# RMS norm and matmul on one core: TensorE's program as two pages, with a first pass through both

## The chip, the cores and the metric

The kernel runs on one core of a Trainium2 chip. The metric is the device time of one execution in microseconds (us). The profile is one execution taken by the hardware profiler; its span runs from the first to the last profiled instruction.

The engines are TensorE (PE; PEld is its weight load, which overlaps with products), VectorE (DVE), ScalarE (ACT), GpSimd (POOL) and SyncE (SP), whose queue issues nearly all transfers. Sixteen DMA engines carry them; each transfer is split over all sixteen.

## The reference

```
batch, seq, dim, out_dim = 16, 1024, 512, 768
rms = sqrt(mean(x ** 2, axis=-1, keepdims=True) + eps)
x_norm = x / rms * gamma
return matmul(x_norm, weight)
```

x has 16,384 rows of 512 floats (33.6 MB), the output 16,384 rows of 768 (50.3 MB). All is float32.

## The kernel before

**Tiles.** A tile is 128 rows, and there are NT = 128 tiles, worked in NP = 64 pairs j. x is loaded in groups of up to 16 tiles into two buffers xt, the results leave from three buffers ot in stores of up to 8 tiles. For each pair:

- POOL casts x to bf16 (`cast`, line 251, into xb; `cast_quad`, line 326, into xq).
- ACT squares and sums the rows (`square`, line 258) and takes the root; DVE forms the reciprocal (`root`, line 265).
- The tiles have to be turned so that features lie across the partitions. Six pairs of eight are turned on PE (`transpose_word`, line 292: four words of 128x128 for a pair, into PSUM tp) and copied out by DVE (`evac`, line 301, into xT). The last two pairs of each group of eight, from pair 14 on, are turned by DVE alone (`move_quad`, line 342, sixteen moves, three at a time, into xTq). Pairs 6 and 7 are turned on PE, too, but land in xTq.
- PE multiplies by the weights, which gamma has been folded into (`matmuls`, line 373: four weight loads and eight products a tile). Between the products `feed` puts the transposes of a later pair (`feeder`, line 396, with a list of how many words follow each of the eight weight loads).
- `finish_tile` (line 385) scales by the reciprocal on its way out of PSUM, the even tile of a pair on ACT, the odd one on DVE, and `store` (line 355) issues the transfer once the tiles of a store are there.

**Order of issue.** Nothing is scheduled by a tool. Every operation is recorded with `run` or `order.transfer` in the order in which the code stands, and `Order.emit` (line 37) then works out which waits each one needs, gives out semaphores and issues it on its engine. The main loop over pairs (line 473) lists loads, casts, norms, products.

PE's instructions as the built program has them, transposes counted as a weight load and a product: 240 in the opening, 242 in the loop, 49 behind it.

## Time and profile before

| what | value |
|---|---|
| median of 3 runs (lowest to highest) | 209.61 us (209.57 to 210.52) |
| the profiled execution, its own time | 210.62 us |
| its span | 208.8 us |
| bytes read from and written to HBM | 35.13 MB, 50.33 MB |
| last products on PE end, last eviction starts | 199.40 us, 199.44 us |
| a turn of PE's loop (eight pairs) | 23.4 us |

How to read it: the page gives busy time by engine, the span in 40 equal slices with the busy share in tenths, the DMA queues (q1 carries the kernel's transfers, the queues of the kind "instruction" the loading of program pages), and groups of instructions by line. The views by stretches give busy time of PE, PEld, DVE, ACT and POOL, the granted clock of PE, the mean busy share of the DMA engines and what they moved. A mean over DMA engines does not tell whether all of them work; how far apart they are is read from the landing records, sixteen for each transfer.

### The profile page before, as it was taken

Reading aid. Unit: us, or ns where it says so; the run is one execution under the profiler, and the core shown is the slowest. Engines: PE = TensorE matmul, PEld = TensorE weight load, DVE = VectorE, ACT = ScalarE, POOL = GpSimd, SP = SyncE. Lnnn points to the kernel's source line nnn. Section 1 sums busy time; section 2 is a strip of 40 time slices with the busy share of each in tenths; the row PEclk is TensorE's granted clock in tenths of the full one; section 3 lists DMA queues with packets and bytes.
Section 4 is the critical chain, followed back from the end, with each engine's and each line's share of the span. In section 5 each row is a group of like instructions: output and inputs, shape, how many; then the busy total and the mean of one; then the engine's idle time right before and its main releaser. Section 6 shows DMA issues by size and latency. Waiting matters only on the chain.

```text
span 208.8 us, 2821 instructions
## 1 busy us (share of the span) xinstructions
PE 194.5 (93%) x1236; PEld 72.7 (35%) x717; DVE 149.4 (72%) x255; ACT 146.2 (70%) x363; POOL 59.8 (29%) x34
## 2 busy tenths in 40 slices
PE   7789979999999999999999999999999999999910
PEld 1234433443344333342344333443333334433200
DVE  0455645999569975999469984999569984999410
ACT  4698888677877498774977787677877688673310
POOL 3147633009300093004900651006700265000000
PEclk9999999999999999999999999999999999999995
DMA  6999999999999999999999999999999999999991
GB/s 227 426 439 430 377 385 430 477 405 430 405 388 414 369 438 424 454 402 449 428 413 446 408 450 428 414 438 425 443 433 414 452 408 438 438 433 400 420 414 78
DMA packets 5628, 85.55 MB, mean 410 GB/s; under 512 B 626, under 2 KB 628, under 8 KB 1780
## 3 DMA queue, kind: packets, MB, share of 16 engines
q1 hardware_dynamic: 5616, 85.46, 97.4%
q8 instruction: 3, 0.05, 0.1%
q14 instruction: 5, 0.04, 0.0%
q10 hardware_dynamic: 4, 0.00, 0.0%
HBM read 35.13 MB, written 50.33 MB: 409 GB/s over the span
## 4 chain that ended last, share of the span: by engine, by line
PE 71%; DMA 15%; DVE 6%; issue 2%; SPq 1%; ACT 1%; POOL 1%; ACTq 0%
PE ps L367 62%; DMA xt<-in_x_dram 15%; PE ps L296 8%; DVE ot L350 2%; DVE xTq L340 2%; DVE xT L309 1%; POOL xb L254 1%; ACT jk L262 0%; SPq L416 0%; SPq L243 0%; ACT ot L348 0%; DVE xTq L309 0%; SPq L360 0%; DVE rstd L269 0%; SPq L544 0%
## 5 line engine op out<-in xcount | busy, mean ns | idle before, releaser
L367 PE MATMUL ps<-w_bf,xT 128*128 128x512 bf16 (+1 forms) x768 | 141.8, 326 | 1.4 <-DVE w_bf L350 0.9
L348 ACT ACTIVATE ot<-ps,rstd 128x768 f32<-128x768 f32 x64 | 57.4, 897 | 42.4 <-PE ps L367 41.2
L262 ACT ACTIVATE jk<-xt 128x512 bf16<-128x512 f32 x128 | 78.7, 618 | 6.9 <-DMA xt<-in_x_dram 6.9
L254 POOL CAST xb<-xt 128x2048 bf16<-128x2048 f32 (+3 forms) x21 | 46.2, 2218 | 114.5 <-DMA xt<-in_x_dram 95.7
L350 DVE TENSOR_SCALAR ot<-ps,rstd 128x768 f32<-128x768 f32 x64 | 64.8, 1013 | 9.0 <-PE ps L367 8.4
L363 PEld LDWEIGHTS <-xT 128*128 128x128 bf16 x384 | 37.7, 98 | 58.2 <-issue 56.9
L296 PE MATMUL ps<-ident_f,xb 128*128 128x128 f32 x200 | 54.2, 275 | 0.9 <-POOL xb L254 0.9
L340 DVE STREAM_TRANSPOSE xTq<-xq 32x256 f32<-32x256 f32 x112 | 48.8, 435 | 3.4
L367 PE MATMUL ps<-w_bf,xTq 128*128 128x512 bf16 (+1 forms) x256 | 49.0, 326 | 1.2 <-DVE xTq L309 1.2
L309 DVE COPY xT<-ps 128x1024 bf16<-128x1024 bf16 (+1 forms) x51 | 33.1, 652 | 23.1 <-PE ps L296 21.5
L296 PEld LDWEIGHTS ps<-ident_f,xb 128*128 128x128 f32 x200 | 28.4, 143 | 46.2 <-issue 42.9
L262 ACT ACTIVATION_READ_ACCUMULATOR jk<-xt 128x1 f32 x128 | 24.3, 190 | 0.0
L363 PEld LDWEIGHTS <-xTq 128*128 128x128 bf16 x128 | 12.5, 98 | 17.8 <-issue 16.1
L329 POOL CAST xq<-xt 128x2048 bf16<-128x2048 f32 x7 | 13.3, 1893 | 0.0
L269 DVE RECIPROCAL rstd<-rms 128x8 f32<-128x8 f32 (+3 forms) x20 | 3.9, 193 | 8.0 <-ACT rms L267 7.8
L267 ACT ACTIVATE rms<-ssq,eps_sb 128x8 f32<-128x8 f32 (+3 forms) x20 | 6.0, 300 | 0.6
L367 PE MATMUL ps<-warm 128*128 128x512 bf16 x10 | 4.4, 578 | 1.4 <-DVE eps_sb L425 1.4
L394 ACT ACTIVATE told<-eps_sb 128x1 f32<-128x1 f32 x20 | 3.8, 192 | 0.0
L309 DVE COPY xTq<-ps 128x1024 bf16<-128x1024 bf16 x2 | 1.4, 692 | 2.4 <-PE ps L296 2.4
L348 ACT ACTIVATE w_bf<-w_f,g_sb 128x768 bf16<-128x768 f32 x2 | 1.9, 935 | 1.5 <-DMA w_f<-in_weight_dram 0.9
L446 DVE COPY g_sb<-ps 128x4 f32<-128x4 f32 x1 | 0.2, 161 | 3.2 <-PE ps L440 3.2
L412 ACT ACT_TABLE_LOAD x1 | 1.3, 1283 | 1.5 <-SPq L503 1.5
(12 smaller groups left out, 3.6 us busy)
## 6 DMA issues: line engine op xcount, KB each, us to landing
out_dram<-ot SPq DMA_DIRECT2D x13, 3072.0 KB, 16.3
xt<-in_x_dram SPq DMA_DIRECT2D x9, 2048.0 KB, 21.0
xt<-in_x_dram SPq DMA_DIRECT2D x3, 4096.0 KB, 22.1
out_dram<-ot SPq DMA_DIRECT2D x4, 1536.0 KB, 12.0
out_dram<-ot SPq DMA_DIRECT2D x3, 768.0 KB, 8.2
w_f<-in_weight_dram SPq DMA_DIRECT2D x2, 768.0 KB, 5.7
xt<-in_x_dram SPq DMA_DIRECT2D x2, 512.0 KB, 5.2
xt<-in_x_dram SPq DMA_DIRECT2D x1, 1024.0 KB, 9.2
```

The source lines that it names most:

```text
L254: run(POOL, lambda: POOL.tensor_copy(out=xb[s][:, i % 8:i % 8 + n, :], in_=src), of, cells("xb", s, i % 8, n))
L262: run(ACT, lambda: ACT.activation(out=jk[j], in_=src[:, 0, :], func=AF.Square, accum_out=ssq[:, i:i + 1]), of, [("jk", j), ("ssq", i)])
L267: run(ACT, lambda: ACT.activation(out=rms[:, s], in_=ssq[:, s], func=AF.Sqrt, scale=1.0 / D, bias=eps_sb), [("ssq", t) for t in range(i, i ...
L269: run(DVE, lambda: DVE.reciprocal(out=rstd[:, s], in_=rms[:, s]), [("rms", i)], [("rstd", t) for t in range(i, i + n)])
L296: run(PE, lambda: PE.transpose(out=tp[b][:, t, h, :], in_=words[:, lo:lo + P], identity=ident_f), cells("xb", s, j % 4 * 2 + t) + ["ident" ...
L309: run(DVE, lambda: DVE.tensor_copy(out=dst[:, t:t + n, :], in_=src[:, t:t + n, :]), [("tp", b)], to[t:t + n])
L329: run(POOL, lambda: POOL.tensor_copy(out=xq[s], in_=src), of, [("xq", s)])
L340: run(DVE, lambda: DVE.transpose(out=dst, in_=src), [("xq", s)], ["xTq"])
L348: run(ACT, lambda: ACT.mul(out=dst, in_=src, mul=r), reads, writes)
L350: run(DVE, lambda: DVE.tensor_single_scalar(out=dst, in_=src, scalar=r, op=mybir.AluOpType.mult), reads, writes)
L363: run(PE, lambda: PE.ldweights(lhsT), [cell])
L367: run(PE, lambda: PE.add_instruction(mybir.InstMatmult(name=nc.get_next_instruction_name(), engine=mybir.EngineType.PE, ins=[PE.lower_ap(r ...
```

## The change

- **The loop begins at pair 4 and takes in the last pair.** Its turns are pairs 4 to 11, 12 to 19 and so on, and the last one is only its first half, pairs 60 to 63: a counter `turn` is compared in the middle of each turn, and the last turn leaves there. Nothing stands behind the loop.
- **Opening.** It now holds pairs 0 to 3 only. So that the loop's body is the same in each turn, pairs 3 and 4 are transposed during pair 2, pairs 5, 6 and 7 (12 words) during pair 3, and no words during pairs 4 and 5.
- **Transposes at the end.** Pairs 62 and 63 feed pairs 64 and 65, which don't exist: the words of an old xb are transposed, and not copied out.
- **Two stand-ins.** A memset of one column on POOL at pair 60 and one on DVE at pair 5 are recorded as if they wrote xb and xTq, so that each turn has the same waits.
- **A first pass.** All of PE's program lies in an outer loop of two passes. In the first, `seen` is 0: it branches past the opening, then past the loop to the code behind it, and back. In the second it runs both.
- **Warm-up.** The first warm-up of PE has five products instead of six.

Before has 240, 242 and 49 PE instructions in the three parts; after has 182 in the opening (with its branch), 113 and 130 in the loop's two halves, and four in what follows.

```
@@ Order.emit
-        assert all([h for _, h in self.body[t]] == [h for _, h in self.body[turns[0]]] for t in turns)
-        waits = [sorted({place[d][0] for t in turns for d in needs[self.body[t][q][0]]}) for q in range(size)]
+        middle = sum(h == 0 for _, h in self.body[turns[0]])
+        assert all([h for _, h in self.body[t]] == [h for _, h in self.body[turns[0]]] for t in turns[:-1])
+        assert [h for _, h in self.body[turns[-1]]] == [0] * middle
+        waits = [sorted({place[d][0] for t in turns for d in needs[self.body[t][q][0]]} if q < middle else
+                        {place[d][0] for t in turns[:-1] for d in needs[self.body[t][q][0]]}) for q in range(size)]
...
-            q = next(q for q in range(final + 1, size) if q not in flags and q not in taken and self.ops[self.body[turns[0]][q][0]][0] == "product")
+            q = next(q for q in range(final + 1, (middle, size)[half]) if q not in flags and q not in taken and self.ops[self.body[turns[0]][q][0]][0] == "product")
...
-        behind = max(spot)
-        late = [n for n in outer if n > behind and self.ops[n][1] is nc.tensor]
+        only = [mybir.EngineType.PE]
+        opening = [n for n in outer if self.ops[n][1] is nc.tensor]
+        assert max(opening) < min(spot)
         for n in outer:
-            if n < len(self.ops) - 1 and n not in late:
+            if n < len(self.ops) - 1 and self.ops[n][1] is not nc.tensor:
                 give(n)
-        with nc.Fori(0, len(turns), engines=[mybir.EngineType.PE], head_slot={mybir.EngineType.PE: 0}):
-            for q, (n, half) in enumerate(self.body[turns[0]]):
-                for who in waits[q]:
-                    nc.tensor.wait_ge(own[who, half], values[q, who])
-                ins = self.ops[n][2]()
...
-        for n in late:
-            give(n)
+
+        def part(name, above):
+            nc.switch_body(name, parent=above, valid_engines=only)
+
+        seen, turn = (nc.alloc_registers(name, engines=only) for name in ("seen", "turn"))
+        nc.regs_mov(seen, 0)
+        with nc.Fori(0, 2, engines=only):
+            above = nc.cur_bb.parent
+            nc.br_lt(seen, 1, on_true="past_opening", on_false="opening", engines=only)
+            part("opening", above)
+            for n in opening:
+                give(n)
+            nc.br("past_opening", engines=only)
+            part("past_opening", above)
+            nc.br_lt(seen, 1, on_true="past_turns", on_false="turns", engines=only)
+            part("turns", above)
+            nc.regs_mov(turn, 0)
+            with nc.Fori(0, len(turns), engines=only, head_slot={mybir.EngineType.PE: 0}):
+                within = nc.cur_bb.parent
+                for q, (n, half) in enumerate(self.body[turns[0]]):
+                    if q == middle:
+                        nc.br_lt(turn, len(turns) - 1, on_true="second_half", on_false="past_turns", engines=only)
+                        part("second_half", within)
+                    for who in waits[q]:
+                        nc.tensor.wait_ge(own[who, half], values[q, who])
+                    ins = self.ops[n][2]()
...
+                nc.regs_alu(turn, turn, 1, op=mybir.AluOpType.add)
+            nc.br("past_turns", engines=only)
+            part("past_turns", above)
+            nc.regs_alu(seen, seen, 1, op=mybir.AluOpType.add)
@@ feeder
-                elif (t, h) == (1, 1):
+                elif (t, h) == (1, 1) and j < NP:
                     evac(j)
@@ ahead of the pairs
-    warm_up(6)
+    warm_up(5)
@@ the loop over pairs
-    mid, one, two, both = ([0, 0, 1, 1, 0, 1, 1, 0], [1, 1, 0, 1, 1, 0, 0, 0], [1, 0, 1, 0, 1, 0, 1, 0],
-                           [1, 1, 1, 1, 1, 1, 1, 1])
+    mid, two, both, most = ([0, 0, 1, 1, 0, 1, 1, 0], [1, 0, 1, 0, 1, 0, 1, 0], [1, 1, 1, 1, 1, 1, 1, 1],
+                            [2, 1, 2, 1, 2, 1, 2, 1])
...
+        elif j % 8 == 4:
+            run(POOL, lambda: POOL.memset(warm[:, :1], 0.0), [], cells("xb", 0, 0, 8))
...
+        elif j == 5:
+            run(DVE, lambda: DVE.memset(warm[:, :1], 0.0), [], ["warm", "xTq"])
...
-        if j < 3:
-            feed = feeder([j + 1], mid if j == 1 else one, alone=j == 1)
+        if j == 1:
+            feed = feeder([2], mid, alone=True)
+        elif j == 2:
+            feed = feeder([3, 4], both)
         elif j == 3:
-            feed = feeder([4, 5], both)
-        elif j + 2 < NP and quad_of(j + 2) is None:
+            feed = feeder([5, 6, 7], most)
+        elif (j + 2) % 8 < 6:
             feed = feeder([j + 2], two)
...
-        order.turn, order.half = ((j - 6) // 8, (j - 6) % 8 // 4) if 6 <= j < NP - 2 else (None, 0)
+        order.turn, order.half = ((j - 4) // 8, (j - 4) % 8 // 4) if 4 <= j else (None, 0)
```

More of the change, by code (lines that the diff above doesn't have):

```diff
@@ L93, in emit @@
         for t in turns:
-            for half in range(2):
+            for half in range(2 if t != turns[-1] else 1):
                 for who in range(len(engines)):
@@ L116, in emit @@
         flags = {spot[d][1] for d in awaited if d in spot}
-        awaited |= {self.body[t][q][0] for t in turns for q in flags}
+        awaited |= {self.body[t][q][0] for t in turns for q in flags if q < len(self.body[t])}
         seen = {who for clock in known for who in clock}
@@ L145, in give @@
                 ins.then_inc(own[place[n][0], events[n][1]], 1)
-        behind = max(spot)
-        late = [n for n in outer if n > behind and self.ops[n][1] is nc.tensor]
+        only = [mybir.EngineType.PE]
+        opening = [n for n in outer if self.ops[n][1] is nc.tensor]
+        assert max(opening) < min(spot)
         for n in outer:
-            if n < len(self.ops) - 1 and n not in late:
+            if n < len(self.ops) - 1 and self.ops[n][1] is not nc.tensor:
                 give(n)
-        with nc.Fori(0, len(turns), engines=[mybir.EngineType.PE], head_slot={mybir.EngineType.PE: 0}):
-            for q, (n, half) in enumerate(self.body[turns[0]]):
-                for who in waits[q]:
-                    nc.tensor.wait_ge(own[who, half], values[q, who])
-                ins = self.ops[n][2]()
-                if n in marks:
-                    ins.then_inc(marks[n][0], 1)
-                elif q in taken:
-                    ins.then_inc(*taken[q])
@@ L161, in emit @@
-        for n in late:
-            give(n)
+        def part(name, above):
[22 more added lines that the diff above has]
+                    ins = self.ops[n][2]()
+                    if n in marks:
+                        ins.then_inc(marks[n][0], 1)
+                    elif q in taken:
+                        ins.then_inc(*taken[q])
+                nc.regs_alu(turn, turn, 1, op=mybir.AluOpType.add)
+            nc.br("past_turns", engines=only)
+            part("past_turns", above)
+            nc.regs_alu(seen, seen, 1, op=mybir.AluOpType.add)
```

## The prediction

> **What bounds the kernel now.** I read the page's shares and DMA lines first, then stretches of the span side by side, then TensorE's waits, then the DMA lines of three short stretches. By share PE looks like the bound (93% busy), but the transfers say otherwise.

> ```profile
> PE 194.5 (93%) x1236; PEld 72.7 (35%) x717; DVE 149.4 (72%) x255; ACT 146.2 (70%) x363; POOL 59.8 (29%) x34
> ...
> DMA  6999999999999999999999999999999999999991
> ...
> q1 hardware_dynamic: 5616, 85.46, 97.4%
> q8 instruction: 3, 0.05, 0.1%
> q14 instruction: 5, 0.04, 0.0%
> ```

> The sixteen DMA engines are full from the second slice to the last but one. Whole stretches run at some 430 GB/s, so 85.46 MB need 199 us, and the first data packet starts at 1.97 us (the trace's packet records). That leaves 208.8 - 201 = 8 us not accounted for. The next view (columns: stretch, its length, busy us of each engine, clock, DMA share, GB/s) shows where it is:

> ```profile
> 24.00:26.00 2.00, 2.00 (x15) 0.74 (x8) 0.99 (x2) 2.00 (x6) 1.50 (x1) 1.00 0.95 262
> 26.00:28.00 2.00, 2.00 (x15) 0.81 (x8) 0.62 (x1) 2.00 (x6) 0.00 (x0) 1.00 0.81 308
> ...
> 56.00:60.00 4.00, 4.00 (x28) 1.52 (x15) 2.58 (x4) 3.01 (x10) 0.00 (x0) 1.00 1.01 367
> ...
> 100.00:150.00 50.00, 50.00 (x327) 19.00 (x189) 39.37 (x66) 39.02 (x98) 18.66 (x9) 1.00 1.01 430
> ...
> 200.00:202.00 2.00, 0.00 (x0) 0.00 (x0) 0.46 (x1) 0.00 (x0) 0.00 (x0) 1.00 1.01 421
> 202.00:204.00 2.00, 0.00 (x0) 0.00 (x0) 0.00 (x0) 0.00 (x0) 0.00 (x0) 0.94 0.88 366
> 204.00:206.00 2.00, 0.00 (x0) 0.00 (x0) 0.00 (x0) 0.00 (x0) 0.00 (x0) 0.50 0.29 123
> 206.00:209.00 3.00, 0.00 (x0) 0.00 (x0) 0.00 (x0) 0.00 (x0) 0.00 (x0) 0.50 0.07 31
> ```

> Against 431 GB/s the dips cost 1.35 us in 24-28 and 0.6 us in 56-60. The tail matters more: from 204 on the DMA share is 0.29, then 0.07, so a few engines still work while most are done. A store is complete only when all sixteen have written their part. In the trace's records of the last store ten engines finish between 203.6 and 203.9 us, the other six at 204.64, 205.11, 205.88, 206.93, 207.40 and 207.56. **The end is set by the slowest DMA engine, 3.7 us behind the ten.**

> Following the same records back: up to the load that lands at 21.4 us no engine is over 0.5 us behind. In the load landing at 27.2 one is 2.0 us late; at 35.0 us two are 1.3 late; the pair stays together, 2.3 at 70, 3.2 at 119, 4.1 at 193. A third falls back slowly from about 80 us: its 24,576-byte packets of the stores take some 945 ns, the others' 912. TensorE's page loads fall into the same stretches. The first one stands at the loop's entry; PE's wait there (released by, us in total, times, longest) and the timeline around it:

> ```profile
> PE ps L367 <- DVE xTq L309: 1.2, 1, 1.2
> ...
> 28.04 0.69 DVE L309 COPY xTq<-ps 128x1024 bf16<-128x1024 bf16 x1 [1.42 <-PE ps L296]
> ...
> 29.52 0.50 PE L367 MATMUL ps<-w_bf,xTq 128*128 128x512 bf16 x2 [1.19 <-DVE xTq L309]
> ```

> The three packets of q8 are at 27.02, 33.03 and 194.14 us in the trace's records, 16,384 bytes each, 0.95 to 1.08 us long. The first two match the two laggards; after the third a new engine appears 1.8 us late. At the loop's entry PE is idle 1.19 us: the copy it is said to wait for ends at 28.73, yet PE resumes only at 29.52.

> **The change part by part.** The sum is made against the profiled execution: 210.62 us, of which 208.8 are span; the median of the runs, 209.61, is 1.01 lower, and I carry gains over to it.

> *Fewer page loads in the full stretch.* Before, 240 instructions of opening, then the loop's page, then 49 of late work. After, 182 of opening and one page that holds the loop, its exit and the end. The loads at 27.02 and 33.03 go, or move to about 1 us, ahead of the first x packets at 1.97. If both leaders of the queue of laggards lose their lag, the third sets the end, 206.93: 207.56 - 206.93 = **-0.63 us**. Bounds: 0, if an early load puts an engine as far behind, since nothing later lets it catch up; -3.7, if the others' lag goes as well. The load at 194.14 delays an engine that ends at 205.11 and is worth nothing by itself.

> *Loop entry.* The 1.19 us of PE go: pairs 6 and 7 are transposed at pair 3 already, and the loop starts at pair 4. PE is not the end, and the covering work is the DMA's backlog. Where PE's pace does reach DMA is early: the store issued at 50.11 comes 1.5 us before the one ahead of it lands (51.65), and DMA dips after it. An earlier store can close the dip at 56-60: **-0.6 us**. Bounds 0 (another cause) and -2.9 (this dip, the one at 24-28, and 1.0 us at 66-70, 324 GB/s). I take the one dip because it is the only one that follows a late store.

> *Dead transposes.* In the last half turn pairs 62 and 63 now feed pairs 64 and 65, which don't exist: 8 transposes at 0.108 us (their step between two products, 27.73 to 27.84) = 0.86 us on PE, nobody reads them. PE's net is -1.19 + 0.86, so the last eviction (199.44) moves by about -0.3. Cover: the lagging engines' backlog of 3.7 us. Without it the ten engines would be bare: the last store, issued at 200.8, plus 1.03 us from issue to first packet (x load, 0.94 to 1.97) plus 8 packets of 0.23 us ends at 203.7, just their end now. So 0, at most +0.9.

> *First pass.* Register moves and some six branches before the warm-up, which waits for VectorE until 1.40. Lower bound 0: five warm products instead of six give back 2.74/6 = 0.46 us. Upper bound of one page wait: 27.02 to 29.52 = 2.5 us. Then the warm-up starts at 3.9, gamma's transposes at 6.2 instead of 4.07, the weights' scaling at 7.0 instead of 6.62, the first product 0.4 late, and PE's waits for casts at 10.66 and 13.2 (0.9 us) absorb it. [...]

> [...]

> *The rest.* Pair 3 carries 12 transposes; pair 6's first needs the cast of tiles 12 to 15, which ends at 20.67 (16.94 + 3.73), about when it comes: 0 to 0.5 us, before DMA runs short. The two memsets sit in idle time of VectorE (23.1 us idle ahead of its copies) and GpSimd (29% busy). The compare in the middle of each turn lies in PE's queue like the back edge, which shows no gap now: 0. The other queues keep their order.

> Sum: 210.62 - 0.63 - 0.6 = 209.4 for the profiled execution, 209.61 - 1.23 = **208.4 us** for the median.

> **The rivals.** *The lag only changes its owner (no change).* The page loads of the first pass fall on engines that are about to be full for 200 us, their lag grows as the pair's did, and the dips have another cause. For it: one load made 2.0 us of lag, and the pair's later growth (2.3 to 4.1) has no page load beside it. Against: before 1.97 us engines are empty. Time 209.61, give or take 0.5.

> [...]

> *The whole tail goes.* If the third laggard exists only under the profiler and the other lags shrink too, the end comes 2.7 to 3 us earlier: 206.7.

> **How the numbers follow.** Forecast 0.34, whole tail 0.08, no change 0.33, first pass 0.25. A measurement of this kernel can tell about 0.5%, or 1.05 us: faster means below 208.56. So faster 0.42, same 0.33, slower 0.25. The forecast's own range is 207.5 to 209.2; to hold 8 in 10 it reaches to most of both sides, 206.9 to 211.3.

> **What would show it.** Right: no 16,384-byte instruction packet between 5 and 190 us; no idle at the loop's first product; in the tail, fewer engines after 205 us (share in the two stretches before the end lower, span shorter). Wrong: PE's first product after 8.5 us; page loads still in the full stretch; a tail as long as before with other engines in it; or a DMA rate that changes in the middle, where I have no term.

## The result, and the profile after

| | median, us | lowest to highest |
|---|---|---|
| before | 209.82 | 209.57 to 210.52 |
| after | 212.62 | 212.49 to 212.86 |

The ratio is 1.0129, with a 95% interval of 1.0102 to 1.0157: the changed kernel is slower by 2.8 us. The forecast was 208.4 us, with a range that ended at 211.3; both the sign and the range missed. The profiled execution of the changed kernel took 212.86 us, with a span of 210.9. A trace is one execution: that of the kernel before took 210.62 us, 0.8 above its median, so traces are compared place by place and times by their medians.

The page of the kernel after, shares, DMA slices and queues:

```profile
PE 195.4 (93%) x1243; PEld 73.6 (35%) x725; DVE 149.4 (71%) x256; ACT 146.3 (69%) x363; POOL 60.0 (28%) x35
...
DMA  6999999997999999999999999999999999999686
...
q1 hardware_dynamic: 5616, 85.46, 96.6%
q14 instruction: 5, 0.04, 0.0%
q8 instruction: 1, 0.02, 0.0%
```

The page loads of q8 did fall from three to one, as predicted; the packet of the one left starts at 3.68 us and takes 0.95. The five smaller loads of q14 stay. The kernel moves the same 85.46 MB. What is new are two notches in the DMA row: a 7 in the tenth slice and a 6 in the third from the end. The stretches of the kernel after around these places (stretch, length, busy us of PE, PEld, DVE, ACT, POOL, clock, DMA share, GB/s):

```profile
51.00:53.00 2.00, 2.00 (x15) 0.59 (x6) 1.90 (x4) 1.49 (x4) 2.00 (x2) 1.00 0.16 66
100.00:150.00 50.00, 49.64 (x322) 18.64 (x185) 40.12 (x68) 39.45 (x99) 18.59 (x8) 1.00 1.00 428
...
198.00:201.00 3.00, 3.00 (x21) 1.20 (x12) 1.02 (x1) 0.96 (x2) 0.00 (x0) 1.00 0.20 82
...
207.00:209.00 2.00, 0.00 (x0) 0.00 (x0) 0.00 (x0) 0.00 (x0) 0.00 (x0) 0.70 0.94 387
...
209.00:210.90 1.90, 0.00 (x0) 0.00 (x0) 0.00 (x0) 0.00 (x0) 0.00 (x0) 0.50 0.02 6
```

The same two stretches of the kernel before:

```profile
51.00:53.00 2.00, 2.00 (x15) 0.59 (x6) 1.49 (x3) 1.52 (x4) 2.00 (x2) 1.00 0.95 397
...
198.00:201.00 3.00, 1.40 (x9) 0.29 (x3) 1.02 (x1) 0.99 (x2) 0.00 (x0) 1.00 1.00 420
```

In between nothing changed: 428 GB/s against 430. But from 51 to 53 us and from 198 to 201 the engines now stand nearly empty, 1.7 and 2.4 us lost as a mean over the sixteen. The long tail of stragglers is gone, too: 0.94 in 207 to 209 and then 0.02, where before it trickled out at 0.29 and 0.07. That is no gain, as the experiments show; the punctual engines were made to wait for work.

Three delays of PE lead to the first empty stretch. PE's waits in the kernel after (released by, us in total, times, longest):

```profile
PE ps L394 <- issue: 2.5, 1, 2.5
PE ps L323 <- POOL xb L281: 2.1, 3, 1.2
PE ps L394 <- DVE w_bf L377: 1.2, 2, 0.8
```

The wait for `xTq` at the loop's entry, 1.19 us before, isn't among them: that part of the change works. In its place stand a later start (1.4 us before), a longer wait for the scaled weights (0.9 before in total), and a longer wait for casts (0.9 before). The timeline of the kernel after (start, duration, in brackets the idle time ahead and its releaser), first of 2.4 to 8.1 us:

```profile
2.47 2.31 PE L394 MATMUL ps<-warm 128*128 128x512 bf16 x5 [2.47 <-issue]
...
7.46 0.75 DVE L377 TENSOR_SCALAR w_bf<-w_f,g_sb 128x512 bf16<-128x512 f32 x2 [0.17 <-DMA w_f<-in_weight_dram]
7.52 0.94 ACT L375 ACTIVATE w_bf<-w_f,g_sb 128x768 bf16<-128x768 f32 x1 [1.66 <-DMA w_f<-in_weight_dram]
8.00 0.38 PE L394 MATMUL ps<-w_bf,xT 128*128 128x512 bf16 x1 [0.82 <-DVE w_bf L377]
```

The same scaling and the same product in the kernel before:

```profile
6.62 0.74 DVE L350 TENSOR_SCALAR w_bf<-w_f,g_sb 128x512 bf16<-128x512 f32 x2
...
7.15 1.51 PE L367 MATMUL ps<-w_bf,xT 128*128 128x512 bf16 x8 [0.60 <-DVE w_bf L350]
```

The scaling is released by the weights' transfer, not by gamma, and starts at 7.46 and 7.52 where it started at 6.62 and 6.44 before. Call the lag of a transfer the time from the median of its sixteen landings to the last one. The lag is 1.6 us in the transfer that lands at 5.82, just after the page load, still 1.6 at 21.3 and 2.3 at 27.4; before, it was not over 0.5 up to 21.4. The records name no engine; that one and the same engine is late is read from how steady the lag is. Tile 0 leaves PSUM at 12.17 instead of 11.10. Then the timeline of 17.9 to 21 us:

```profile
17.99 3.74 POOL L281 CAST xb<-xt 128x2048 bf16<-128x2048 f32 x2 [2.85 <-DMA xt<-in_x_dram]
...
19.95 0.33 PE L323 MATMUL ps<-ident_f,xb 128*128 128x128 f32 x1 [1.25 <-POOL xb L281]
```

Two casts, the first done about 19.9: it brings tiles 8 to 11, and tiles 8 and 9 are pair 4. The new opening transposes pair 4 in pair 2, and PE stands for 1.25 us until that cast is there. In what follows, lateness is how much later a tile's eviction starts than in the kernel before: 1.06 us at tile 0, 3.58 at tile 5, 4.50 at tile 7. The loop then gives back 2.24 of it, as its entry has no stall and pairs 4 and 5 carry no words, and the lateness is 2.26 at tile 16 and 2.21 at tile 100. The store of tiles 16 to 23 is issued at 52.4 instead of 50.11, and the x load behind it in SP's queue at 52.74 instead of 50.49: the engines run dry at 51. From 61.7 us on the punctual engines land everything 2.0 us later than before.

The second empty stretch is in the tail, in the timeline of 197 to 202.7 us:

```profile
199.48 1.02 DVE L377 TENSOR_SCALAR ot<-ps,rstd 128x768 f32<-128x768 f32 x1 [2.02 <-PE ps L394]
...
200.53 0.81 SPq L387 DMA_DIRECT2D out_dram<-ot  x2
...
202.52 1.02 DVE L377 TENSOR_SCALAR ot<-ps,rstd 128x768 f32<-128x768 f32 x1 [2.02 <-PE ps L394]
```

The eviction from 196.45 to 197.47 finishes tile 123, the last one that the store of tiles 120 to 123 needs. Yet this store is issued at 200.53, when the eviction of tile 125 (199.48 + 1.02) is over, together with the store of tiles 124 and 125. In the kernel before it left at 195.28, as the eviction of tile 123 (194.24 + 1.02) ended:

```profile
194.24 1.02 DVE L350 TENSOR_SCALAR ot<-ps,rstd 128x768 f32<-128x768 f32 x1 [0.62 <-PE ps L367]
```

```profile
195.28 0.33 SPq L360 DMA_DIRECT2D out_dram<-ot  x1
```

This is a new wait. An operation that a product inside PE's loop waits for raises a semaphore kept for PE (`own`); whoever else needs it is told by the next instruction of that engine that is not such a one (`shared`). Before, pairs 62 and 63 stood behind the loop and waited on the ordinary signals. Now they are in it, and the signal for tile 123 comes with tile 125's eviction.

### The profile page after: what moved, and what is told of

It reads as the page before. It is cut to its first block, busy times and chain, and to the rows that moved or that the text cites. A ratio compares the mean times of both kernels' runs of the same rounds, so it can differ in the third digit from the quotient of the medians.

```text
span 210.9 us, 2859 instructions
## 1 busy us (share of the span) xinstructions
PE 195.4 (93%) x1243; PEld 73.6 (35%) x725; DVE 149.4 (71%) x256; ACT 146.3 (69%) x363; POOL 60.0 (28%) x35
## 3 DMA queue, kind: packets, MB, share of 16 engines
q1 hardware_dynamic: 5616, 85.46, 96.6%
## 4 chain that ended last, share of the span: by engine, by line
PE 68%; DMA 18%; DVE 7%; SPq 1%; issue 1%; POOL 1%; ACT 1%; ACTq 0%
PE ps L394 60%; DMA xt<-in_x_dram 18%; PE ps L323 8%; DVE ot L377 3%; DVE xTq L367 2%; DVE xT L336 1%; POOL xb L281 1%; SPq L270 1%; ACT jk L289 0%; SPq L443 0%; ACT ot L375 0%; DVE xTq L336 0%; SPq L387 0%; DVE rstd L296 0%; SPq L577 0%
## 5 line engine op out<-in xcount | busy, mean ns | idle before, releaser
L375 ACT ACTIVATE ot<-ps,rstd 128x768 f32<-128x768 f32 x64 | 57.5, 899 | 44.7 <-PE ps L394 44.7
L323 PE MATMUL ps<-ident_f,xb 128*128 128x128 f32 x208 | 56.0, 276 | 3.0 <-POOL xb L281 2.1
L367 DVE STREAM_TRANSPOSE xTq<-xq 32x256 f32<-32x256 f32 x112 | 48.8, 435 | 3.4
L394 PE MATMUL ps<-w_bf,xTq 128*128 128x512 bf16 (+1 forms) x256 | 49.9, 326 | 0.0
L323 PEld LDWEIGHTS ps<-ident_f,xb 128*128 128x128 f32 x208 | 29.5, 143 | 49.9 <-issue 43.8
L296 DVE RECIPROCAL rstd<-rms 128x8 f32<-128x8 f32 (+3 forms) x20 | 3.9, 193 | 7.7 <-ACT rms L294 7.5
L394 PE MATMUL ps<-warm 128*128 128x512 bf16 x9 | 3.9, 571 | 2.5 <-issue 2.5
## 6 DMA issues: line engine op xcount, KB each, us to landing
xt<-in_x_dram SPq DMA_DIRECT2D x3, 4096.0 KB, 21.4
```

Of the source, the lines that this page charges most:

```text
L296: run(DVE, lambda: DVE.reciprocal(out=rstd[:, s], in_=rms[:, s]), [("rms", i)], [("rstd", t) for t in range(i, i + n)])
L323: run(PE, lambda: PE.transpose(out=tp[b][:, t, h, :], in_=words[:, lo:lo + P], identity=ident_f), cells("xb", s, j % 4 * 2 + t) + ["ident" ...
L367: run(DVE, lambda: DVE.transpose(out=dst, in_=src), [("xq", s)], ["xTq"])
L375: run(ACT, lambda: ACT.mul(out=dst, in_=src, mul=r), reads, writes)
L394: run(PE, lambda: PE.add_instruction(mybir.InstMatmult(name=nc.get_next_instruction_name(), engine=mybir.EngineType.PE, ins=[PE.lower_ap(r ...
```

## The experiments

All medians and ratios stand beside runs of the kernel before on the same chip. e1, e2, e6 and e10 are edits of the kernel after, e4, e8 and e12 of the kernel before, and e3, e5, e7, e9 and e11 of the kernel after without its first pass.

| kernel | median, us | ratio to before, 95% | lateness at tile 16, us |
|---|---|---|---|
| after | 212.62 | 1.0129 (1.0102 to 1.0157) | 2.26 |
| e1 tail | 212.9 | 1.0143 (1.0110 to 1.0177) | 2.38 |
| e2 words | 211.79 | 1.0093 (1.0059 to 1.0127) | 1.29 |
| e3 no pass | 211.54 | 1.0088 (1.0053 to 1.0124) | 0.92 |
| e4 before, with a pass | 215.69 | 1.0258 (1.0207 to 1.0309) | 5.37 |
| e5 no pass, words | 211.12 | 1.0060 (1.0040 to 1.0080) | 0.16 |
| e6 early loads | 213.04 | 1.0153 (1.0136 to 1.0170) | 2.20 |
| e7 no pass, late start | 211.53 | 1.0079 (1.0057 to 1.0102) | 1.15 |
| e8 before, dead words | 209.88 | 1.0003 (0.9981 to 1.0025) | 0.24 |
| e9 no pass, words, tail | 210.85 | 1.0065 (1.0044 to 1.0085) | 0.01 |
| e10 early loads, tail | 210.67 | 1.0042 (1.0024 to 1.0059) | |
| e11 all of these | 209.97 | 1.0012 (0.9996 to 1.0027) | 0.16 |
| e12 before, early loads | 209.95 | 1.0008 (0.9990 to 1.0025) | -0.97 |

The one profiled execution of e10 took 213.27 us, against 209.62 to 211.45 for its other twelve, and had tile 0 2.55 us late, so only e10's times are read.

**e1: the new wait of the tail taken out.** A memset of one column on VectorE behind the evictions of tiles 123 and 125 passes the signal on at once (the one behind tile 125 has nothing to pass on, as that store had left with tile 125's own signal).

```
+    told_d = sb("told_d", [P, 1], F32)
@@ finish_tile
+        if engine is DVE and i in (NT - 5, NT - 3):
+            run(DVE, lambda: DVE.memset(told_d, 0.0), [], ["told_d"])
```

> The changed kernel, plus one tiny memset on VectorE right after the eviction of tile 123 and after that of tile 125, so that the stores of tiles 120 to 123 and of 124 and 125 have an instruction to wait for that comes at once. Theory (a new wait: inside the loop an eviction counts for TensorE, so a store can only wait for the next VectorE instruction, which for tile 123 is the eviction of tile 125, 3.0 us later, and DMA runs empty from 198.3 to 201.6 us): the store of 120 to 123 is issued near 197.5 instead of 200.53, the gap closes, and the time falls by 2 to 3 us to 209.6 to 210.6. Rival (TensorE's own end, 3.1 us later than before, sets the time): the last eviction stays at 202.5, the time falls by less than 0.5 us, to 212.1 or more.

The stretches of e1:

```profile
51.00:53.00 2.00, 2.00 (x14) 0.64 (x7) 1.90 (x4) 1.40 (x4) 2.00 (x2) 1.00 0.10 41
...
198.00:201.00 3.00, 3.00 (x21) 1.22 (x12) 1.02 (x2) 0.99 (x2) 0.00 (x0) 1.00 0.99 418
...
206.00:208.00 2.00, 0.00 (x0) 0.00 (x0) 0.00 (x0) 0.00 (x0) 0.00 (x0) 0.50 0.47 190
```

The empty stretch at 198 to 201 is gone (0.20 to 0.99), and nothing was gained, 212.9 us. The stragglers are back: the landings of the last store spread again, the twelfth of sixteen at 207.1 and the last at 211.0. In the kernel after the lag is 3.9 us in the store that lands at 198.6, so the slowest engine was still at work until 202.57, while the others idled. Filling the others' idle time doesn't help the one that ends last. An estimate from the landings agrees: in the kernel before 7.34 us pass from the last landing of the store issued at 191.19 (200.55) to the end of the stores (207.89). The last landing of the same store is at 202.57 in the kernel after and at 203.62 in e1, which makes 209.9 and 211.0; measured are 209.98 and 211.0. My expectation took the gap's full price; the gap is real, the price is zero while the slowest engine is what ends.

**e2: pair 4's words late in pair 2.** Pair 4's four words (transposes) move behind the last of pair 2's eight weight loads; pair 3's stay spread among them.

```
-            feed = feeder([3, 4], both)
+            feed = feeder([3, 4], [1, 0, 1, 0, 1, 0, 1, 4])
```

> The changed kernel with pair 4's four transposes put behind the last product of pair 2 instead of between its last products (gaps 1,0,1,0,1,0,1,4 instead of eight times 1). Theory (those words wait for the cast of tiles 8 and 9 until 19.9 us, hold up three product groups behind them, and TensorE's 2.2 us of lateness let DMA run empty near 52 us): TensorE's wait for the cast falls from 1.25 us to 0.5 or less, tile 16's eviction comes at most 1.7 us after that of the kernel before instead of 2.26, and the time falls by 0.4 to 0.8 us to 211.8 to 212.2. Rival (the cast is late anyhow and the words only move): 212.6.

A wait of PE in e2, and then a stretch of it:

```profile
PE ps L323 <- POOL xb L281: 1.2, 3, 0.6
```

```profile
51.00:53.00 2.00, 2.00 (x15) 0.59 (x6) 1.90 (x4) 1.67 (x5) 2.00 (x2) 1.00 0.60 250
```

The wait for casts fell from 2.1 us in total to 1.2, the longest from 1.2 to 0.6, and tile 16's lateness by 0.97 to 1.29. The first empty stretch is half filled (0.16 to 0.60), and the time fell by 0.83. So the wait for the cast of tiles 8 and 9 is a cause, with about that size.

**e3: no first pass.** The opening stands once ahead of the loop; the loop and its exit in mid-turn stay.

```
-        nc.regs_mov(seen, 0)
-        with nc.Fori(0, 2, engines=only):
-            nc.br_lt(seen, 1, on_true="past_opening", on_false="opening", engines=only)
...
+        for n in opening:
+            give(n)
+        nc.regs_mov(turn, 0)
+        with nc.Fori(0, len(turns), engines=only, head_slot={mybir.EngineType.PE: 0}):
```

> The changed kernel without its first pass: opening, then the loop, once. Theory (the page load at 3.68 us puts one DMA engine 1.6 us behind, so every early load lands 1.07 us late): no page load before 20 us, first product at 7.15 instead of 8.00, tile 0's eviction 1.07 us earlier, tile 16 at most 1.3 us later than before instead of 2.26; page loads come back into the full stretch. The end still has the late stores, so the time falls by 0.5 to 1.2 us to 211.4 to 212.1. Rival (the pass costs only TensorE's later start, 2.46 instead of 1.40, and the lag of early loads is by chance): tile 0 stays 0.8 to 1.1 us late, 212.6.

The timeline of e3 at its first product of tiles, and a stretch of it:

```profile
7.10 0.75 PE L385 MATMUL ps<-w_bf,xT 128*128 128x512 bf16 x3 [0.67 <-DVE w_bf L368]
```

```profile
51.00:53.00 2.00, 2.00 (x15) 0.59 (x6) 1.90 (x4) 1.52 (x6) 2.00 (x2) 1.00 0.99 410
```

The first product comes at 7.10 instead of 8.00, tile 0 is 0.32 us early instead of 1.06 late, tile 16 gains 1.34, the first empty stretch is full, and the time falls by 1.08. The one page load left is at 28.65 us, in the full stretch, and does there what it did at 3.68: the lag goes from 0.5 us in the transfer that lands at 28.5 to 1.5 in the next. At 197.6 us it is 3.6.

**e7: the late start alone.** On e3, the warm-up waits for an operation of ScalarE, so that it starts at 3.03 us, later than with the pass (2.47).

```
+    run(ACT, lambda: ACT.mul(out=told, in_=eps_sb, mul=1.0), ["eps"], ["told", "warm"])
     warm_up(5)
```

> The changed kernel without its first pass, but with TensorE's warm-up made to wait for a ScalarE instruction behind the table load, so that it starts at 2.9 us instead of 1.4: the late start of the first pass without its early page load. Theory (the page load and not the late start makes the early loads land late): tile 0's eviction at most 0.4 us later than without the wait (10.8), the time within 0.5 us of 211.5. Rival (the late start does it): tile 0 at 11.8 or later, 212.3 or more.

The start cost 0.27 us at tile 0 against e3 and nothing in time (211.53 against 211.54). Its first product comes at 8.31, later than the changed kernel's 8.00, and still tile 0 is 0.05 us early against the kernel before. So the pass does not cost by making PE late. What is left, in the records, is its page load at 3.68 us and the DMA engine that falls behind right after it; in e7 the load comes at 28.68, and the lag goes from 0.4 to 1.8 us there. A kernel with an early page load and no pass was not built.

**e4: the pass on the old program.** The opening, loop and late part of the kernel before inside the same outer loop of two passes.

```
+        with nc.Fori(0, 2, engines=only):
+            nc.br_lt(seen, 1, on_true="past_opening", on_false="opening", engines=only)
...
+            nc.br_lt(seen, 1, on_true="past_turns", on_false="turns", engines=only)
```

> The kernel before with the first pass alone: its opening, loop and late part in an outer loop of two passes, of which the first branches past them. Theory (an early page load on one engine delays all early loads): tile 0's eviction about 1.1 us late, the store near 50 us about 1 us late, DMA short of work there by up to 1 us: 210.3 to 211.0 us. Rival (a page load early is cheaper than one in the full stretch, so the pass by itself gains): 208.8 to 209.6 us.

A wait of PE in e4, and a stretch of it:

```profile
PE ps L388 <- issue: 8.5, 1, 8.5
```

```profile
52.00:56.00 4.00, 4.00 (x27) 1.27 (x14) 3.77 (x8) 3.40 (x9) 3.90 (x3) 1.00 0.17 70
```

PE does nothing until 8.54 us. Page loads lie at 3.86, 4.63 (1.9 us long) and 11.34. The direction was expected, the size was not: 215.69 us against the 210.3 to 211.0 of the theory. With tile 16 5.37 us late, the engines stand nearly empty for 4 us (0.17). Why PE stands until 8.54 here and only until 2.47 in the changed kernel is open: the records don't say which page a load brings, and three loads is what the kernel before has without a pass.

**e5: no pass, and pair 4's words late** (e2 and e3 together).

> The changed kernel without its first pass and with pair 4's words behind pair 2's last product (both edits of the earlier runs together). Theory (the two delays add up, and the time follows TensorE's lateness at tile 16, plus some 0.7 us that the end costs): tile 16's eviction within 0.3 us of the kernel before, time 210.2 to 210.8. Rival (the two share one wait, so that either edit alone brings all there is): tile 16 still 0.8 us or more late, 211.4 or more.

Tile 16 is 0.16 us late, as expected, and at 51 to 53 the DMA share is 1.07. But 211.12 us is above the 210.2 to 210.8 I gave. Being on time in the opening is not all: the share at 198 to 201 is only 0.60, with the tail's wait still there (the store of tiles 120 to 123 leaves at 198.74, against 195.28 before).

**e9: the tail's signal as well** (e1, e2 and e3 together).

> The changed kernel without first pass, with pair 4's words behind pair 2's last product and with the stores of the last turn waiting for a memset of their own: all three repairs. Theory (two bounds lie close together: the slowest DMA engine's own work, and the late store of tiles 120 to 123 plus the 3.1 MB behind it; a repair shows only when both move): the early lateness is gone (tile 16 within 0.4 us), the last landings no longer lie together, and the time comes to within 0.5 us of the kernel before, 209.4 to 210.3. Rival (the store's wait is worth nothing, as the run with that repair alone had it): 210.9 or more, as without the third repair (211.12).

210.85 us, above the 209.4 to 210.3 expected. Both stretches are full (1.08 and 1.02), tile 16 is on time (0.01), and 1 us is still missing. The step from e5 (0.27 us) is inside the intervals. The trace cannot show the missing time: it is of e9's fastest execution, 210.42 us, and its last landing, 207.55, is earlier than the 207.89 of the kernel before.

**e6: loads freed from the late stores.** From tile 48 on the x load goes into SP's queue four pairs earlier, ahead of the store that it stood behind.

```
-        load_until((2 * j + AHEAD + XG - 1) // XG * XG)
+        if j == 7:
+            load_until(3 * XG)
...
+        if j >= 11 and j % 8 == 3:
+            load_until(2 * j + 26 + XG)
```

> The changed kernel with each load of x from tile 48 on put four pairs earlier into SyncE's queue, ahead of a store that it now stands behind (issued from the point where its buffer is free). Theory (TensorE's 2.26 us of lateness costs time only because all but one of the DMA engines run empty near 52 us, where the store is late and the load stands behind it): TensorE stays 2.2 us late at tile 16, the empty stretch near 52 us goes, and the time falls by 1 to 2 us to 210.6 to 211.6. Rival (the end of the kernel is TensorE's own end): the empty stretch goes and the time stays at 212.3 or more.

The stretches of e6:

```profile
51.00:53.00 2.00, 2.00 (x14) 0.59 (x6) 1.90 (x4) 1.54 (x4) 2.00 (x3) 1.00 1.10 475
...
192.00:194.00 2.00, 2.00 (x14) 0.59 (x6) 1.90 (x4) 0.90 (x1) 0.00 (x0) 1.00 0.40 166
197.00:199.00 2.00, 2.00 (x15) 0.82 (x8) 0.32 (x1) 0.99 (x2) 0.00 (x0) 1.00 0.37 154
199.00:201.00 2.00, 2.00 (x15) 0.84 (x9) 1.02 (x1) 0.14 (x1) 0.00 (x0) 1.00 0.00 0
```

The stretch at 51 is full, and the time is 213.04: no gain, which was the rival's number. DMA now runs ahead of PE, and its idle time has moved to the end, 0.40, 0.37, then 0.00. All waits for the last stores: from the same wait as in the kernel after they are issued at about 200.5, one us goes by to the first packet (0.94 to 1.97 before), and 3.1 MB (eight tiles) at 431 GB/s need 7.3, which makes 208.9 at best.

**e10: early loads and the tail's signal** (e1 and e6 together).

> The changed kernel with its first pass and its early lateness, but with the loads moved ahead in SyncE's queue and the stores of the last turn waiting for their own memset: each of the two edits alone gained nothing. Theory of the two bounds: with no empty stretch near 52 us the slowest engine is through early, and with the store of tiles 120 to 123 issued near 197.6 instead of 200.6 nothing holds the end: 3 to 2 us less than 213, 209.6 to 211.0, with TensorE still 2.2 us late at tile 16. Rival (TensorE's lateness is the time): 212.3 or more.

e1 alone gained nothing, e6 alone gained nothing, both together take 1.95 us: 210.67. That is the sign of two bounds that lie side by side: the slowest engine's backlog, which is smaller in e6 (its last landing of the store issued near 193.3 is at 199.94, against 202.57 in the kernel after), and the late last stores, which e1 moves forward. Either alone holds the end where it is. What e6 saves the slowest engine isn't the empty stretch: in the kernel after its landings there are 7.29 us apart (55.10 and 62.39), the time of a 3.1 MB store at 431 GB/s, so it did not idle. The records show slow packets right behind: around 59.7 us 15 store packets of 24,576 bytes, close to one for each engine, take 1.4 to 1.8 us instead of 0.91. Each of the ten traced kernels without early loads has 12 to 16 packets over 1.3 us like this between 57 and 63 us; e6, e11 and e12, with them, have none. Why they are slow is open.

**e11: everything** (e1, e2, e3 and e6 together).

> All three repairs and the loads moved ahead. Theory: TensorE on time, no late store and no empty stretch, so only the slowest engine's own work is left, which the kernel before has as well: 209.0 to 210.0, no better than 0.5 us against the kernel before. Rival (moving the loads takes work off the end, since the stores then have the engines to themselves): below 209.0, better than both kernels.

The stretches of e11:

```profile
51.00:53.00 2.00, 2.00 (x14) 0.59 (x6) 1.65 (x3) 1.52 (x4) 2.00 (x2) 1.00 1.03 438
...
199.00:201.00 2.00, 2.00 (x16) 0.83 (x9) 0.49 (x2) 0.99 (x2) 0.00 (x0) 1.00 0.95 399
```

209.97 us, ratio 1.0012 with an interval that holds 1: the time of the kernel before. Its loop still begins at pair 4, still ends in mid-turn and still has the dead transposes, so with early loads those parts cost nothing that can be measured, and gain nothing either. Without early loads (e9) 1.05 us against the kernel before stays unexplained.

**e12: early loads in the kernel before.** The edit of e6 on the kernel before.

> The kernel before with the loads of x from tile 48 on moved four pairs ahead in SyncE's queue. Between the changed kernel's repaired forms this edit went with a gain of 0.9 us (210.85 to 209.97). Theory (its gain is the closing of stretches in which DMA engines wait for a store, and the kernel before has none before its end): within 0.5 us of the kernel before, 209.3 to 210.3. Rival (it also shortens the slowest engine's work, in any kernel): 208.5 to 209.2, faster than both.

A stretch of e12, the dip in which I had looked for a gain (0.6 us at 367 GB/s before):

```profile
56.00:60.00 4.00, 4.00 (x28) 1.73 (x17) 2.54 (x5) 2.43 (x7) 0.00 (x0) 1.00 1.02 442
```

The dip is gone, and the time is 209.95, the same. So the early loads are no improvement of their own. In the changed kernel they do buy time, 0.88 us from e9 to e11, although e9 is on time at tile 16; what they buy back there is not known.

**e8: dead transposes in the kernel before.** Pairs 62 and 63 of the kernel before feed words that nobody reads.

```
-        elif j + 2 < NP and quad_of(j + 2) is None:
+        elif (j + 2) % 8 < 6 or j < 6:
...
-                elif (t, h) == (1, 1):
+                elif (t, h) == (1, 1) and j < NP:
```

> The kernel before with the eight unused transposes of pairs 64 and 65 put among the products of pairs 62 and 63. Theory (the slowest DMA engine has some 3.7 us of work left behind the others at the end and hides TensorE's 0.87 us): time within 0.4 us of the kernel before. Rival (the end follows TensorE): 0.7 to 0.9 us more.

209.88 us, ratio 1.0003: the last eviction is 1.47 us late, 0.87 of it by the eight transposes (tile 122 is 0.60 late), and it costs nothing.

## Why the prediction was wrong, point by point

**"Fewer page loads in the full stretch", -0.63 us: wrong.** The loads went as predicted; the lag did not go with them. Around 195 us the lag is 3.8 to 3.9 us in the kernel before with three page loads, 3.8 to 3.9 after with one, at the start, 3.2 to 3.6 in e7 and e3 with one at 28.7, and 4.0 to 4.1 in e4 with three early ones; e11 and e12 reach 3.9 and 4.4 at 180. I had matched two laggards to two packets by their times, and left the growth from 2.3 to 4.1 with no load of q8 beside it to a rival. So the term's step from fewer loads to less lag at the end failed: the lag rises by 1.0 to 1.5 us beside the load at 3.68 us (after), 27.02 (before) and 28.7 (e3, e7), but the lag at the end does not follow the loads. What builds it up is open. The rival "the lag only changes its owner" was right in this.

**"Loop entry", -0.6 us by way of an earlier store: wrong in sign.** The 1.19 us of stall went. But PE was late by more than that when it got there, so the store at 50.11 came 2.3 us later instead of earlier. The condition I had named, DMA running thin behind a late store, came true in the changed kernel (share 0.16 at 51 to 53) and worked against it. The dip that I wanted to close was something else: my own row has the engines at a share of 1.01 from 56 to 60 us, so they had work, and what was slow were packets (13 of 1.4 to 1.8 us at 57.5 to 58.2). The gain it was to bring does not exist even when the dip is closed (e12).

**"First pass", taken as 0: wrong.** I had priced PE's delay, up to a page wait of 2.5 us, and found it absorbed. PE started at 2.47, within that bound, and e7 shows that this alone does cost nothing. What I left out is that with the pass the page load comes in the first microseconds (3.68 us, against 28.65 in e3), where the weights and the first x loads are short and awaited, and each of them lands in sixteen parts. With one landing 1.6 us behind the weights were late, with them the first product by 0.85 (8.00 against 7.15), and tile 0 by 1.06. e3 prices the pass at 1.08 us of time. The chance "first pass 0.25" stood for a slower kernel, and slower it is; but the first product came at 8.00, ahead of the 8.5 that was to prove the forecast wrong, and the only page load started at 3.68, after PE had started, so no row shows a second load. The store and the load behind it came 2.3 us late, and that was not regained.

That PE's program is two pages is my count, which no run shows. The records have the loads of 16,384 bytes, one in the changed kernel and three in e4: PE starts at 2.47 us with the one and at 8.54 with the three, and what it waited for until then they don't say. How much of the 1.07 us by which PE starts later than in the kernel before (2.47 against 1.40) goes to the branches, no row shows.

**"The rest", 0 to 0.5 us for pair 3's words: wrong place.** I checked the cast that pair 6 needs and did not check pair 4, whose words moved from pair 3 into pair 2: the cast of tiles 8 and 9 ends at about 19.9, and PE waits 1.25 us. e2 prices it at 0.83 us of time.

**"The other queues keep their order": true and not enough.** The order is the same, but a signal changed its carrier, and the store of tiles 120 to 123 left at 200.53, 3 us after its last eviction. This term was missing altogether. By itself it costs nothing (e1); once the backlog is shortened it decides (e10 against e6: 2.4 us).

**"Dead transposes", 0: right** (e8, 1.0003), for the reason given, the slowest engine's backlog. **"Set by the slowest DMA engine": right** for the kernel before; after, the late stores and that engine end together: the last store's sixteen landings lie within 0.8 us, 209.21 to 209.98.

Of the 2.80 us, then, taking out the pass and the early words leaves 1.32 (e5), the signal on top of that 1.05 (e9), and the early loads 0.17 (e11), each against the 209.80 of the kernel before beside it. That last step, 0.88 us, is outside both intervals, but its cause was not isolated: in e9 the eviction of the last tile is 1.36 us late and both stretches are full. The parts don't add in any order, since the two bounds cover for each other. No version tried is faster than the kernel before.

## What to carry to other kernels

Before a wait is taken out, ask of every step moved earlier whether its data is there by then, one by one, the small steps too; and ask of every operation moved into a loop with its own semaphores who else was listening to its signal. Where transfers are split over all DMA engines, read the end from the slowest one, and read a dip in GB/s together with the share: at 56 to 60 us of the kernel before, 367 GB/s at a share of 1.01 were slow packets and no lack of work. Filling the others' idle time was worth nothing here while the slowest one ended last (e1: share 0.20 to 0.99, 212.9 us), and with a late store beside it neither cure showed alone (e1 212.9, e6 213.04, both together 210.67), so try both together before calling either harmless. Look at where a load of program code falls: with it at 3.68 us, while the weights were awaited, tile 0 was 1.06 us late, with it at 28.7 0.32 early (e3).

## What the runs showed of the hardware

- A 16,384-byte page load (0.95 us at 3.68) was followed by one of sixteen landings coming 1.6 us late, still so at 21.3 us, in transfers of sixteen landings each. In e3 and e7 the load at 28.7 us was followed by a lag that rose from 0.5 and 0.4 us to 1.5 and 1.8.
- One landing ends up 3.2 to 4.7 us behind the median after some 195 us of full traffic in the kernels without early loads, with three page loads, one early, or one in the middle. In every trace 107 to 146 of the 1,664 store packets of 24,576 bytes take 920 to 1,000 ns, 942 to 947 on average, instead of 912. An engine's share is 104 packets; if one engine has them, that makes an estimated 3.4 us, which the records, without engine names, don't settle.
- At 57 to 63 us 12 to 16 of these packets take over 1.3 us, in all kernels whose x load stands behind the store there, and in none whose load stands ahead of it (e6, e11, e12); why, the runs leave open.
- The longer program, with three page loads, had PE start at 8.54 us when it was stepped through in a first pass (e4), the shorter one, with one load, at 2.47. Without a pass PE starts at 1.40 (before) and 1.39 (e3).
